# A hybrid decoder layer on one core: all x tiles loaded first, low parts of the k, v and u weights on GpSimd, k normed with a scaled epsilon, and the opening in written order

## The chip, the cores and the metric

The program runs on one core of a Trainium2 chip. A core has five engines that run their own instruction streams side by side: TensorE (PE in the profile; PEld is its weight load), VectorE (DVE), ScalarE (ACT), GpSimd (POOL) and SyncE (SP), which issues the DMAs here. They meet only at semaphores. The time is device microseconds of the whole launch, as the median of three runs.

## The reference, cut to what matters

One layer of a decoder on x of 1024 positions by 1024 features, in float32:

```python
h = rmsnorm(x, mix_norm)
q, k, v, su, sv, g_a, g_b = split(h @ w_in)          # 512,128,128,512,512,1024,1024 columns
y_att = sliding_window_attention(q, k, v, q_norm, k_norm, sinks)   # 8 query heads, 2 kv heads of 64
y_sgu = chunked_spatial_gating(su, sv, sgu_norm, w_s, b_s)
x = x + (sigmoid(g_a)*(y_att @ w_oa) + sigmoid(g_b)*(y_sgu @ w_ob)) @ w_out
x = x + conv_gated_mlp(rmsnorm(x, ffn_norm), w_up, conv_w, conv_b, w_down)
# inside the attention, per head of 64:
q = q * rsqrt(mean(q*q) + 1e-6) * q_norm
k = k * rsqrt(mean(k*k) + 1e-6) * k_norm
```

The change touches only the opening: the k and v columns of the projection, the norm of x (a row sum of squares), the norm of k, the first four query blocks, and what is prepared for the first scores.

## The kernel before, in words

**Float32 by three products.** Every operand is split into a high part, rounded to the matmul type (`copy_hi`, an ACT copy, line 89), and a low part, the rest (a subtraction on DVE or GpSimd). `mm3` (lines 91 to 95) then issues three matmuls: high by high, high by low, low by high.

**The x stage (lines 197 to 255).** x comes transposed in eight tiles of 128 features, k = 0 to 7. A tile `xr[k]` holds one column of gains, the 256 weight columns of k and v, and 1024 positions: 640.5 KB, loaded by `xload` on SP's queue. For each tile, ACT rounds the weights to `wkv` high and the gained x to `x` high in two halves; the low parts are line 230 (weights, DVE) and line 234 (x, DVE, a scalar_tensor_tensor that reads `xf` or `xr` and the high part). Then 24 matmuls of 128x256 add the tile's share of k and v into the two PSUM tiles `pkv`. `xsquare` squares the tile on ACT into PSUM (line 218) and DVE adds it to `sqsum`, which lies in `rstd_b` (line 219). Five tiles are loaded ahead (`X_AHEAD`); tiles 0 to 2 lie in one buffer of the pool `Y` (`xf`), 3 to 7 rotate through three buffers (`xr`). In this stage PE keeps its written order, and the order of the other engines is chosen by a scheduler; SP's queue is in that order too, and it starts with tile 3. Seven small matmuls `warm` run on PE before the first tile.

**Weights of the first queries and of u.** `rsplit` makes the two halves of `wq` (copy on ACT, low part of 128x1024 on GpSimd, line 193). The first tile of u is split at line 258 (ACT) and 259 (DVE).

**From there to the first scores (lines 317 to 420), in written order on all engines.** PE: the row sums of squares (`ssq`, line 321), `q_proj(0)` and `q_proj(1)` (24 matmuls each), four transposes of normed k (`pk`), `q_proj(2)`, transposes of the first two query blocks (`pqt`), the reciprocal norms as a row (`rb`, half 0), `q_proj(3)`, k's other half, `rb` half 1, and the first scores (`sc`, line 439). Beside it DVE and GpSimd make `rstd` (x's reciprocal norm), and from k's squares `kss` the factor `krs`: times `rstd` squared, plus epsilon, to the power -1/2 on GpSimd (line 131), times `rstd` again; line 348 applies it. `q_ms` does it for a query block with the scaled epsilon `eps_x` and no `rstd`: q's raw values carry the factor that cancels. `v_evac` takes v out of PSUM, `v_split` splits it; `k_hi`, `k_lo`, `k_twice` split k.

PSUM tiles of half size (`PH`, four buffers) hold the squares, `ssq`, `pq`, `pk`, `pqt` and `rb` in turn: a new one waits until an older one has been read. A DMA waits until the eighth DMA before it on the queue has landed.

Of the kernel before, what the change touches and what calls it, by code (L numbers as in the profile page):

```python
# [10 lines left out]
F = mybir.dt.float32  # L11
R = mybir.dt.float32r
# [6 lines left out]
D = 1024  # L19
# [3 lines left out]
EPS = 1e-6  # L23
# [5 lines left out]
ROWS = (slice(0, 64), slice(64, 128))  # L29
X_AHEAD = 5  # L30
FILL = "qu|q|qu|qu|uu|q|qu|qu|q|qu|qu|qu|q|uu|u|u|uu|vv|v|v".split("|")
# [10 lines left out]
def body(ctx, tc, nc, a):  # L42
# [157 lines left out]
    xr = {}  # L200
    x_first = Y("xf", F, [128, 3, 1281])

    def xload(k):
        xr[k] = x_first[:, k, :] if k < 3 else pa.tile([128, 1281], F, tag="xr", name=nm("xr"), bufs=3)
        if k == 0:
            nc.sync.dma_start(xr[k][:, 0:513], a["xw"][k, :, 0:513])
            nc.sync.dma_start(xr[k][:, 513:1281], a["xw"][k, :, 513:1281])
        else:
            nc.sync.dma_start(xr[k], a["xw"][k])
# [10 lines left out]

    for k in range(X_AHEAD):
        xload(k)
    warm = PH("warm")
    for _ in range(7):
        nc.tensor.matmul(warm[:, 0:128], rstd_b[:, 0:128], rstd_b[:, 0:128], start=True, stop=True)
    xcuts = {0: (slice(0, 256), slice(256, 512), slice(512, 1024))}
    for k in range(8):
        x1 = xr[k]
        copy_hi(wkv[:, 0, k, :], x1[:, 1:257])
        nc.vector.tensor_tensor(wkv[:, 1, k, :], x1[:, 1:257], wkv[:, 0, k, :].bitcast(F), op=ALU.subtract)  # L230
        for c in xcuts[k] if k in xcuts else (slice(0, 512), slice(512, 1024)):
# [4 lines left out]
        for s in range(8):  # L236
# [3 lines left out]
                k == 0 and s % 2 == 0, k == 7 and s % 2 == 1)  # L240
        if k > 0:
            xsquare(k - 1)
        if k + X_AHEAD < 8:
            xload(k + X_AHEAD)
        if k == 2:
            rwq = rload(a["wq"][0], "wq")
            nc.sync.dma_start(ident, a["ident"])
            nc.sync.dma_start(cp, a["cp"])
        if k == 4:
            u_raw = [wload(a["wu"][0], "wu")]  # L250
            nc.sync.dma_start(sink_b, a["sink"])
            nc.sync.dma_start(ali, a["ali"])
        if k == 5:
            rsplit(wq[0], rwq[0], 0)
    xsquare(7)
    rsplit(wq[0], rwq[1], 1)
    u_next = [wst.tile([128, 8, 128], R, tag="wh", name="u0h"), wst.tile([128, 8, 128], R, tag="wl", name="u0l")]
    copy_hi(u_next[0], u_raw[0])
    nc.vector.tensor_tensor(u_next[1], u_raw[0], u_next[0].bitcast(F), op=ALU.subtract)

# [51 lines left out]
    krs = pa.tile([128, 16], F, name="krs")  # L312
    rstd2 = pa.tile([128, 8], F, name="rstd2")
    kss3 = kss.rearrange("p (s g) -> p s g", g=2)
    krs3 = krs.rearrange("p (s g) -> p s g", g=2)

    man = tc.manual_schedule()
    man.__enter__()
    p_ssq = PH("ssq")
    for s in range(8):  # L320
        nc.tensor.matmul(p_ssq[:, 2 * s:2 * s + 2], sqsum[:, s * 128:(s + 1) * 128], ones,
                         start=True, stop=True)
    q_proj(0)
    q_proj(1)
    ss8 = pa.tile([128, 8], F, name="ss8")
    nc.vector.tensor_scalar(nsink, sink_b, -1.0, None, op0=ALU.mult)
    nc.vector.tensor_scalar(kgq, cp[:, 184:185], cp[:, 185:186], 0.125, op0=ALU.mult, op1=ALU.mult)
    nc.vector.tensor_copy(ss8, p_ssq[:, 0:16].rearrange("p (s two) -> p s two", two=2)[:, :, 0])
    rsqrt_cols(rstd, ss8, 8, D)
    nc.vector.tensor_scalar(eps_x, ss8, EPS / D, EPS * EPS, op0=ALU.mult, op1=ALU.add)  # L330
    ksqs = pa.tile([128, 8, 128], F, tag="sq", name="ksq")
    for h in range(2):
# [3 lines left out]
                                axis=AX.X, op=ALU.add)  # L336
    nc.vector.tensor_tensor(rstd2, rstd, rstd, op=ALU.mult)
    nc.vector.tensor_tensor(kss3, kss3, rstd2.unsqueeze(2).to_broadcast([128, 8, 2]), op=ALU.mult)
    rsqrt_cols(krs[:, 0:8], kss[:, 0:8], 8, 64)
    rsqrt_cols(krs[:, 8:16], kss[:, 8:16], 8, 64)  # L340
    q_sq(0)
    q_sq(1)

    def k_norm(h):
        ss = slice(4 * h, 4 * h + 4)
        nc.vector.tensor_tensor(krs3[:, ss], krs3[:, ss],
                                rstd[:, ss].unsqueeze(2).to_broadcast([128, 4, 2]), op=ALU.mult)
        nc.vector.tensor_tensor(kr[:, ss, :].rearrange("p s (g d) -> p s g d", d=64),
                                pk4[h][:, :, 0:128].rearrange("p s (g d) -> p s g d", d=64),
                                krs3[:, ss].unsqueeze(3).to_broadcast([128, 4, 2, 64]), op=ALU.mult)  # L350
# [38 lines left out]

    v_evac(0)  # L390
    k_norm(0)
    k_trans(0)
    q_ms(0)
    q_ms(1)
    k_hi(0)
    v_evac(1)
    q_norm(0)
# [20 lines left out]
    q_sq(3)
    q_ms(3)
# [1626 lines left out]
```

## Time and profile before

| what | value |
|---|---|
| median of three runs | 1184.44 us (1184.26 to 1184.85) |
| span of the profiled execution, first to last instruction | 1183.5 us |
| median less span | 0.9 us |
| PE busy | 1170.3 us, 99% |
| PE busy from 0 to 80 us | 75.4 us |
| first matmul of the x stage | 6.30 us |
| first matmul of `ssq` (end of the x stage) | 31.41 us |
| first matmul of the scores | 48.93 us |
| mean granted PE clock | 0.998 |

The profile lists the span of its execution and no launch time of its own; the 0.9 us lie before the first and after the last instruction. In the rows below, a timeline row gives start, duration, engine, source line, operation, output and inputs, shapes, count, and in brackets the idle time before it with what ended it. A windows row gives for a stretch of time each engine's busy time and instructions, the granted PE clock, the DMA share and GB/s. Durations of neighbouring instructions on DVE and ACT overlap by some 0.09 us, so that the step from start to start is shorter than the duration.

### The profile page before, as it was taken

What the parts mean: (1) busy time and instruction counts of PE and PEld (TensorE: products, weight loads), DVE (VectorE), ACT (ScalarE), POOL (GpSimd) and SP (SyncE); (2) the same over time, 40 slices, a digit from 0 to 9 for tenths busy, and PEclk for the clock granted to TensorE, in tenths of its full rate; (3) what the DMA queues carried; (4) which work ended last, traced back from release to release, by engine and by line L of the source; (5) the groups of instructions that cost most, each with busy time, mean ns of one, the idle gap of its engine ahead of it and who ended that gap; (6) DMA issues with size and microseconds to landing.
All of it is one profiled execution on the core that took longest, in us unless ns stands there. A gap on an engine that the chain in (4) does not pass through costs nothing.

```text
span 1183.5 us, 15928 instructions
## 1 busy us (share of the span) xinstructions
PE 1170.3 (99%) x5842; PEld 990.4 (84%) x5842; DVE 874.5 (74%) x1037; ACT 566.5 (48%) x878; POOL 631.8 (53%) x435
## 2 busy tenths in 40 slices
PE   8999999999999999999999999999999999999998
PEld 8989989988888878888878888888888888888887
DVE  7798975743536776678788788877888797875674
ACT  8555667644336653335444443444444445425331
POOL 2467685488884764444867677776767541000000
PEclk9999999999999999999999999999999999999999
DMA  7110136157556654454545445455555268975471
GB/s 272 37 55 19 54 130 228 56 168 239 161 160 204 233 193 154 146 176 132 138 129 169 118 149 152 142 141 134 166 137 160 72 219 287 365 232 196 155 231 67
DMA packets 80942, 188.66 MB, mean 159 GB/s; under 512 B 9184, under 2 KB 16864, under 8 KB 80736
## 3 DMA queue, kind: packets, MB, share of 16 engines
q1 hardware_dynamic: 73008, 167.58, 40.7%
q0 software_dynamic: 7456, 15.73, 8.0%
q10 hardware_dynamic: 400, 4.33, 1.1%
q8 instruction: 46, 0.75, 0.3%
q14 instruction: 32, 0.26, 0.1%
HBM read 146.97 MB, written 49.02 MB: 166 GB/s over the span
## 4 chain that ended last, share of the span: by engine, by line
PE 82%; DVE 4%; POOL 3%; ACT 2%; issue 2%; DMA 1%; DVEq 0%; POOLq 0%; SPq 0%; ACTq 0%
PE pz L1060 50%; PE pd L1855 10%; PE pdy L1855 8%; PE px L95 2%; PE px L93 2%; PE px L94 2%; PE pu L95 1%; PE pu L93 1%; PE pu L94 1%; PE pv L517 1%; PE pq L93 1%; PE pq L95 1%; PE pq L94 1%; DVE xa L621 1%; DMA lq<-wup 0%
## 5 line engine op out<-in xcount | busy, mean ns | idle before, releaser
L1060 PE MATMUL pz<-T,qh 128*128 128x512 f32 x472 | 145.6, 390 | 0.0
L1060 PE MATMUL pz<-B,ph 128*128 128x512 f32 x352 | 109.7, 393 | 0.7 <-ACT x L1695 0.7
L1060 PEld LDWEIGHTS pz<-T,qh 128*128 128x128 f32 x472 | 88.4, 188 | 18.6 <-ACT u L885 0.3
L1019 POOL TENSOR_TENSOR pl<-lp,ph 128x1024 fp32r<-128x1024 f32 x30 | 73.2, 2439 | 52.9 <-ACT ph L89 52.9
L1060 PE MATMUL pz<-T,ql 128*128 128x512 f32 x236 | 91.8, 389 | 0.0
L1019 POOL TENSOR_TENSOR ql<-lq,qh 128x1024 fp32r<-128x1024 f32 x30 | 76.8, 2559 | 9.1 <-ACT qh L89 9.1
L1060 PEld LDWEIGHTS pz<-B,ph 128*128 128x128 f32 x352 | 65.1, 188 | 16.7 <-ACT x L1695 3.8
L1078 DVE TENSOR_TENSOR pz<-pz,rstd_b 128x1024 f32<-128x1024 f32 x60 | 73.9, 1232 | 4.6 <-ACT rstd_b L143 2.5
L1060 PE MATMUL pz<-T,s3h 128*128 128x512 f32 x232 | 71.4, 389 | 0.0
L1060 PE MATMUL pz<-y,wjh 128*128 128x512 f32 x224 | 69.5, 391 | 0.6 <-POOL y L1233 0.3
L1060 PE MATMUL pz<-B,pl 128*128 128x512 f32 x176 | 68.6, 390 | 0.0
L1855 PE MATMUL pd<-bh,ah 128*128 128x512 f32 x176 | 68.5, 389 | 0.0
L1855 PE MATMUL pd<-bl,ah 128*128 128x512 f32 x176 | 68.5, 389 | 0.0
L1855 PE MATMUL pd<-bh,al 128*128 128x512 f32 x176 | 68.5, 389 | 0.0
L1060 PE MATMUL pz<-T,AX 128*128 128x512 f32 x264 | 63.4, 389 | 0.0
L1060 PE MATMUL pz<-B,AX 128*128 128x512 f32 x264 | 63.4, 389 | 0.0
L1019 POOL TENSOR_TENSOR s3l<-lq,s3h 128x512 fp32r<-128x512 f32 x20 | 26.0, 1298 | 62.3 <-ACT s3h L89 62.3
L1060 PEld LDWEIGHTS pz<-T,AX 128*128 128x128 f32 x264 | 49.5, 188 | 10.3
L1060 PEld LDWEIGHTS pz<-B,AX 128*128 128x128 f32 x264 | 49.6, 188 | 10.3
L89 ACT ACTIVATE AX<-lr 128x1024 fp32r<-128x1024 f32 x22 | 23.4, 1063 | 70.9 <-POOL lr L621 70.9
L621 DVE TENSOR_TENSOR pz<-pz,u 128x512 f32<-128x512 f32 x37 | 25.9, 700 | 42.5 <-ACT u L1072 36.2
L1550 DVE SCALAR_TENSOR_TENSOR tg<-pz,cp,tg 128x1023 f32<-128x1023 f32 (+1 forms) x44 | 56.2, 1278 | 0.8
(359 smaller groups left out, 3597.6 us busy)
## 6 DMA issues: line engine op xcount, KB each, us to landing
lp<-wup SPq DMA_DIRECT2D x22, 512.0 KB, 3.8
lq<-wup SPq DMA_DIRECT2D x22, 512.0 KB, 4.2
ra<-wdown SPq DMA_DIRECT2D x44, 256.0 KB, 4.9
b<-T SPq DMA_DIRECT2D x44, 256.0 KB, 3.5
lq<-wup POOLq DMA_DIRECT2D x42, 256.0 KB, 5.3
B<-tv SPq DMA_DIRECT2D x33, 256.0 KB, 2.0
T<-tt SPq DMA_DIRECT2D x33, 256.0 KB, 2.1
b<-B SPq DMA_DIRECT2D x33, 256.0 KB, 3.0
```

The source lines that it names most:

```text
L89: return nc.scalar.activation(dst, src, AF.Copy, scale=scale)
L93: nc.tensor.matmul(out, wh, mh, start=first, stop=False, **kw)
L94: nc.tensor.matmul(out, wh, ml, start=False, stop=False, **kw)
L95: nc.tensor.matmul(out, wl, mh, start=False, stop=last, **kw)
L517: nc.tensor.matmul(o, vhl[:, kb, g, :], w[:, 2 * g:2 * g + 2, :], start=i == 0 and g == 0, stop=i == len(ops) - 1, skip_group_check=True)
L621: eng.tensor_tensor(out, x, y, op=op)
L1019: nc.gpsimd.tensor_tensor(l, r, h.bitcast(F), op=ALU.subtract)
L1060: nc.tensor.matmul(o, p[:, k, :], m, start=not more and k == 0 and j == 0, stop=k == nk - 1 and j == 2, skip_group_check=True)
L1078: nc.vector.tensor_tensor(z, z, rstd_b, op=ALU.mult)
L1550: nc.vector.scalar_tensor_tensor(t[:, j:], p[:, 0:1024 - j], cw[:, ci, 2 - j:3 - j], t[:, j:], op0=ALU.mult, op1=ALU.add)
L1855: nc.tensor.matmul(o[d], p[:, k - k0, m], q[:, k - k0, :], start=new and k == 0 and j == 0, stop=k == HK - 1 and j == 2, skip_group_check= ...
```

## The change

- All eight tiles of x are loaded first, in order of k, the first six into two `Y` buffers, the last two into `xr`; then both halves of `wq`, and the small inputs and u's weights that were issued between the tiles.
- Eleven `warm` matmuls in place of seven.
- The low parts of the k and v weights of tiles 1 to 7, and of u's first weights, are made on GpSimd; tile 0's stay on DVE.
- The order of all engines is the written one from the first load on. The squares lag behind the tiles: the last three come after the second half of `wq`.
- `krs` is k's mean square plus `eps_x`, to the power -1/2, with no `rstd` in it: `rstd2` and the product with `rstd` are gone, and `rstd` itself is made later, on GpSimd after the two `krs` powers.
- `q_proj(0)` stands before `ssq`; `v_evac` moves behind the first two query blocks; both `rb` halves stand behind k's second half; u's first copy and subtraction move behind `q_proj(1)` and `v_evac`; the norm and the squares of blocks 2 and 3 stand earlier.

On GpSimd, from the last of the opening's fills on (`wkv` is the k and v weights' low part, `mh` the exponent -1/2). Before:

```order
L172 MEMSET kT_107 64x1024
L193 TENSOR_TENSOR wq_102<-wq_249,wq_102 128x1024
L193 TENSOR_TENSOR wq_102<-wq_251,wq_102 128x1024
L131 TENSOR_TENSOR rstd<-rstd,mh_74 128x8
L131 TENSOR_TENSOR krs<-krs,mh_74 128x8 x2
```

Now (line numbers of the changed kernel):

```order
L171 MEMSET kT_107 64x1024
L239 TENSOR_TENSOR wkv_120<-xf_126,wkv_120 128x256 x2
L239 TENSOR_TENSOR wkv_120<-xf_127,wkv_120 128x256 x3
L192 TENSOR_TENSOR wq_102<-wq_141,wq_102 128x1024
L239 TENSOR_TENSOR wkv_120<-xr_137,wkv_120 128x256
L239 TENSOR_TENSOR wkv_120<-xr_139,wkv_120 128x256
L192 TENSOR_TENSOR wq_102<-wq_143,wq_102 128x1024
L345 TENSOR_TENSOR krs<-krs,mh_74 128x8
L291 TENSOR_TENSOR qss_532<-qss_532,mh_74 128x4
L291 TENSOR_TENSOR qss_545<-qss_545,mh_74 128x4
L397 TENSOR_TENSOR krs<-krs,mh_74 128x8
L130 TENSOR_TENSOR rstd<-rstd,mh_74 128x8
```

The low part of `wq`'s first half now stands ahead of the weights' low parts of tiles 6 (`xr_137`) and 7 (`xr_139`), and the power for `krs` is cut into two with two query powers between them.

On VectorE at tiles 6 and 7. Before (`xr_209` is tile 6, `xr_247` tile 7):

```order
L230 TENSOR_TENSOR wkv_120<-xr_209,wkv_120 128x256
L234 SCALAR_TENSOR_TENSOR x_5_118<-xr_209,x_5_118 128x512
L234 SCALAR_TENSOR_TENSOR x_6_119<-xr_209,x_6_119 128x512
L219 TENSOR_TENSOR rstd_b<-rstd_b,sq_402 128x512
L230 TENSOR_TENSOR wkv_120<-xr_247,wkv_120 128x256
L219 TENSOR_TENSOR rstd_b<-rstd_b,sq_435 128x512
L234 SCALAR_TENSOR_TENSOR x_5_118<-xr_247,x_5_118 128x512
L234 SCALAR_TENSOR_TENSOR x_6_119<-xr_247,x_6_119 128x512
```

Now:

```order
L243 SCALAR_TENSOR_TENSOR x_5_118<-xr_137,x_5_118 128x512
L243 SCALAR_TENSOR_TENSOR x_6_119<-xr_137,x_6_119 128x512
L218 TENSOR_TENSOR rstd_b<-rstd_b,sq_397 128x512
L218 TENSOR_TENSOR rstd_b<-rstd_b,sq_400 128x512
L243 SCALAR_TENSOR_TENSOR x_5_118<-xr_139,x_5_118 128x512
L243 SCALAR_TENSOR_TENSOR x_6_119<-xr_139,x_6_119 128x512
```

The two weight subtractions are gone from DVE, and both additions of one tile's squares stand ahead of tile 7's low parts.

On ScalarE behind the x stage (`ksq` are k's squares, `qsq` those of a query block, `u0h` is u's first high part, `kT` k's). Before:

```order
L89 ACTIVATE wq_102<-wq_251 128x1024
L89 ACTIVATE u0h<-wu_327 128x1024
L334 ACTIVATE ksq<-pkv_124 128x512
L334 ACTIVATE ksq<-pkv_125 128x512
L276 ACTIVATE qsq_537<-pq_469 128x256
L276 ACTIVATE qsq_539<-pq_494 128x256
L89 ACTIVATE kT_107<-pk_544,kgq 64x512 x2
```

Now:

```order
L335 ACTIVATE ksq<-pkv_124 128x512
L335 ACTIVATE ksq<-pkv_125 128x512
L284 ACTIVATE qsq_526<-pq_460 128x256
L284 ACTIVATE qsq_536<-pq_493 128x256
L88 ACTIVATE u0h<-wu_147 128x1024
L88 ACTIVATE kT_107<-pk_540,kgq 64x512 x2
```

The copy of u's weights now stands between the second query block's squares and k's high part.

```diff
@@ -27,7 +27,6 @@
 
 
 ROWS = (slice(0, 64), slice(64, 128))
-X_AHEAD = 5
 FILL = "qu|q|qu|qu|uu|q|qu|qu|q|qu|qu|qu|q|uu|u|u|uu|vv|v|v".split("|")
 WHEN = {"u1": 0, "q0": 1, "q1": 2, "u2": 5, "u3": 9, "v0": 13, "v1": 14, "z0": 16, "z1": 17}
 
@@ -198,10 +197,10 @@
     pkv = [PS("pkv"), PS("pkv")]
     pk4 = [pkv[h].rearrange("p (s c) -> p s c", c=256) for h in range(2)]
     xr = {}
-    x_first = Y("xf", F, [128, 3, 1281])
+    x_first = [Y("xf", F, [128, 3, 1281]) for _ in range(2)]
 
     def xload(k):
-        xr[k] = x_first[:, k, :] if k < 3 else pa.tile([128, 1281], F, tag="xr", name=nm("xr"), bufs=3)
+        xr[k] = x_first[k // 3][:, k % 3, :] if k < 6 else pa.tile([128, 1281], F, tag="xr", name=nm("xr"), bufs=3)
         if k == 0:
             nc.sync.dma_start(xr[k][:, 0:513], a["xw"][k, :, 0:513])
             nc.sync.dma_start(xr[k][:, 513:1281], a["xw"][k, :, 513:1281])
@@ -218,16 +217,26 @@
             nc.scalar.activation(sq, xs, AF.Square)
             nc.vector.tensor_tensor(sqsum[:, c], sqsum[:, c], sq, op=ALU.add)
 
-    for k in range(X_AHEAD):
+    man = tc.manual_schedule()
+    man.__enter__()
+    for k in range(8):
         xload(k)
+    rwq = rload(a["wq"][0], "wq")
+    nc.sync.dma_start(ident, a["ident"])
+    nc.sync.dma_start(cp, a["cp"])
+    u_raw = [wload(a["wu"][0], "wu")]
+    nc.sync.dma_start(sink_b, a["sink"])
+    nc.sync.dma_start(ali, a["ali"])
     warm = PH("warm")
-    for _ in range(7):
+    for _ in range(11):
         nc.tensor.matmul(warm[:, 0:128], rstd_b[:, 0:128], rstd_b[:, 0:128], start=True, stop=True)
     xcuts = {0: (slice(0, 256), slice(256, 512), slice(512, 1024))}
-    for k in range(8):
+
+    def x_block(k):
         x1 = xr[k]
         copy_hi(wkv[:, 0, k, :], x1[:, 1:257])
-        nc.vector.tensor_tensor(wkv[:, 1, k, :], x1[:, 1:257], wkv[:, 0, k, :].bitcast(F), op=ALU.subtract)
+        eng = nc.gpsimd if k else nc.vector
+        eng.tensor_tensor(wkv[:, 1, k, :], x1[:, 1:257], wkv[:, 0, k, :].bitcast(F), op=ALU.subtract)
         for c in xcuts[k] if k in xcuts else (slice(0, 512), slice(512, 1024)):
             xc = x1[:, 257 + c.start:257 + c.stop]
             copy_hi(hx(0, k, c), xc, scale=x1[:, 0:1])
@@ -238,25 +247,24 @@
             c = slice(s * 128, (s + 1) * 128)
             mm3(o, hx(0, k, c), hx(1, k, c), wkv[:, 0, k, :], wkv[:, 1, k, :],
                 k == 0 and s % 2 == 0, k == 7 and s % 2 == 1)
-        if k > 0:
-            xsquare(k - 1)
-        if k + X_AHEAD < 8:
-            xload(k + X_AHEAD)
-        if k == 2:
-            rwq = rload(a["wq"][0], "wq")
-            nc.sync.dma_start(ident, a["ident"])
-            nc.sync.dma_start(cp, a["cp"])
-        if k == 4:
-            u_raw = [wload(a["wu"][0], "wu")]
-            nc.sync.dma_start(sink_b, a["sink"])
-            nc.sync.dma_start(ali, a["ali"])
-        if k == 5:
-            rsplit(wq[0], rwq[0], 0)
-    xsquare(7)
+
+    x_block(0)
+    x_block(1)
+    xsquare(0)
+    x_block(2)
+    x_block(3)
+    xsquare(1)
+    x_block(4)
+    xsquare(2)
+    x_block(5)
+    xsquare(3)
+    rsplit(wq[0], rwq[0], 0)
+    x_block(6)
+    xsquare(4)
+    x_block(7)
     rsplit(wq[0], rwq[1], 1)
-    u_next = [wst.tile([128, 8, 128], R, tag="wh", name="u0h"), wst.tile([128, 8, 128], R, tag="wl", name="u0l")]
-    copy_hi(u_next[0], u_raw[0])
-    nc.vector.tensor_tensor(u_next[1], u_raw[0], u_next[0].bitcast(F), op=ALU.subtract)
+    for k in (5, 6, 7):
+        xsquare(k)
 
     st = {}
 
@@ -310,41 +318,37 @@
     kr = pa.tile([128, 8, 128], F, tag="xr", name="kr", bufs=3)
     kss = pa.tile([128, 16], F, name="kss")
     krs = pa.tile([128, 16], F, name="krs")
-    rstd2 = pa.tile([128, 8], F, name="rstd2")
+    u_next = [wst.tile([128, 8, 128], R, tag="wh", name="u0h"), wst.tile([128, 8, 128], R, tag="wl", name="u0l")]
     kss3 = kss.rearrange("p (s g) -> p s g", g=2)
     krs3 = krs.rearrange("p (s g) -> p s g", g=2)
 
-    man = tc.manual_schedule()
-    man.__enter__()
     p_ssq = PH("ssq")
+    q_proj(0)
     for s in range(8):
         nc.tensor.matmul(p_ssq[:, 2 * s:2 * s + 2], sqsum[:, s * 128:(s + 1) * 128], ones,
                          start=True, stop=True)
-    q_proj(0)
     q_proj(1)
     ss8 = pa.tile([128, 8], F, name="ss8")
-    nc.vector.tensor_scalar(nsink, sink_b, -1.0, None, op0=ALU.mult)
-    nc.vector.tensor_scalar(kgq, cp[:, 184:185], cp[:, 185:186], 0.125, op0=ALU.mult, op1=ALU.mult)
-    nc.vector.tensor_copy(ss8, p_ssq[:, 0:16].rearrange("p (s two) -> p s two", two=2)[:, :, 0])
-    rsqrt_cols(rstd, ss8, 8, D)
-    nc.vector.tensor_scalar(eps_x, ss8, EPS / D, EPS * EPS, op0=ALU.mult, op1=ALU.add)
     ksqs = pa.tile([128, 8, 128], F, tag="sq", name="ksq")
     for h in range(2):
         ksq = ksqs[:, 4 * h:4 * h + 4, :]
         nc.scalar.activation(ksq, pk4[h][:, :, 0:128], AF.Square)
         nc.vector.tensor_reduce(kss[:, 8 * h:8 * h + 8], ksq.rearrange("p s (g d) -> p (s g) d", d=64),
                                 axis=AX.X, op=ALU.add)
-    nc.vector.tensor_tensor(rstd2, rstd, rstd, op=ALU.mult)
-    nc.vector.tensor_tensor(kss3, kss3, rstd2.unsqueeze(2).to_broadcast([128, 8, 2]), op=ALU.mult)
-    rsqrt_cols(krs[:, 0:8], kss[:, 0:8], 8, 64)
-    rsqrt_cols(krs[:, 8:16], kss[:, 8:16], 8, 64)
+    nc.vector.tensor_scalar(nsink, sink_b, -1.0, None, op0=ALU.mult)
+    nc.vector.tensor_scalar(kgq, cp[:, 184:185], cp[:, 185:186], 0.125, op0=ALU.mult, op1=ALU.mult)
     q_sq(0)
+    nc.vector.tensor_copy(ss8, p_ssq[:, 0:16].rearrange("p (s two) -> p s two", two=2)[:, :, 0])
+    nc.vector.tensor_scalar(eps_x, ss8, EPS / D, EPS * EPS, op0=ALU.mult, op1=ALU.add)
+    nc.vector.scalar_tensor_tensor(krs3, kss3, 1.0 / 64, eps_x.unsqueeze(2).to_broadcast([128, 8, 2]),
+                                   op0=ALU.mult, op1=ALU.add)
+    nc.gpsimd.tensor_tensor(krs[:, 0:8], krs[:, 0:8], mh05, op=ALU.pow)
+    q_ms(0)
     q_sq(1)
+    copy_hi(u_next[0], u_raw[0])
 
     def k_norm(h):
         ss = slice(4 * h, 4 * h + 4)
-        nc.vector.tensor_tensor(krs3[:, ss], krs3[:, ss],
-                                rstd[:, ss].unsqueeze(2).to_broadcast([128, 4, 2]), op=ALU.mult)
         nc.vector.tensor_tensor(kr[:, ss, :].rearrange("p s (g d) -> p s g d", d=64),
                                 pk4[h][:, :, 0:128].rearrange("p s (g d) -> p s g d", d=64),
                                 krs3[:, ss].unsqueeze(3).to_broadcast([128, 4, 2, 64]), op=ALU.mult)
@@ -387,13 +391,12 @@
             copy_hi(vh_, vg_)
             nc.vector.tensor_tensor(vl_, vg_, vh_.bitcast(F), op=ALU.subtract)
 
-    v_evac(0)
     k_norm(0)
     k_trans(0)
-    q_ms(0)
     q_ms(1)
+    nc.gpsimd.tensor_tensor(krs[:, 8:16], krs[:, 8:16], mh05, op=ALU.pow)
+    rsqrt_cols(rstd, ss8, 8, D)
     k_hi(0)
-    v_evac(1)
     q_norm(0)
     k_lo(0)
     q_norm(1)
@@ -404,18 +407,21 @@
     q_split(0)
     q_trans(1)
     q_split(1)
-    rms_rows([PH("rb")], rstd, (0,))
+    q_sq(2)
+    q_ms(2)
+    v_evac(0)
+    v_evac(1)
+    nc.gpsimd.tensor_tensor(u_next[1], u_raw[0], u_next[0].bitcast(F), op=ALU.subtract)
     q_proj(3)
     k_trans(1)
+    rms_rows([PH("rb")], rstd, (0,))
     rms_rows([PH("rb")], rstd, (1,))
-    q_sq(2)
+    k_hi(1)
+    q_norm(2)
+    k_lo(1)
+    q_sq(3)
     v_split()
-    q_ms(2)
-    k_hi(1)
-    k_lo(1)
     k_twice(1)
-    q_norm(2)
-    q_sq(3)
     q_ms(3)
     man.__exit__(None, None, None)
     pa_cm.__exit__(None, None, None)
```

## The prediction, made before the run

> **What bounds the kernel now.** I read the busy times first, then stretches of time, then PE's waits.
>
> ```profile
> PE 1170.3 (99%) x5842; PEld 990.4 (84%) x5842; DVE 874.5 (74%) x1037; ACT 566.5 (48%) x878; POOL 631.8 (53%) x435
> 4.40:6.30 1.90, 0.01 (x1) 0.00 (x0) 0.84 (x3) 1.23 (x3) 0.00 (x0) 1.00 1.05 323
> 6.30:8.20 1.90, 1.84 (x9) 1.23 (x9) 0.98 (x4) 1.18 (x3) 0.00 (x0) 1.00 0.90 331
> 8.20:11.60 3.40, 3.40 (x16) 3.40 (x17) 3.02 (x6) 3.40 (x8) 0.00 (x0) 0.50 1.00 405
> 11.60:31.40 19.80, 19.80 (x170) 19.80 (x169) 19.80 (x32) 18.76 (x34) 4.88 (x2) 1.00 0.64 233
> 31.40:49.00 17.60, 16.63 (x143) 16.26 (x141) 11.25 (x30) 6.07 (x12) 6.90 (x5) 1.00 0.18 62
> 130.00:1183.50 1053.50, 1045.81 (x4927) 873.26 (x4925) 766.02 (x808) 484.08 (x652) 564.18 (x361) 1.00 0.53 168
> PE pkv L93 <- ACT x L89: 1.9, 1, 1.9
> PE pqt L295 <- DVE krs L346: 0.6, 1, 0.6
> PE pq L93 <- DVE qs L304: 0.4, 1, 0.4
> ```
>
> PE sets the end: 1170.3 of 1183.5 us are busy, and the order of the work after 60 us is unchanged. So only idle or slow PE time in the opening can be won. The windows show it. From 4.4 to 6.3 PE does nothing (row `pkv`, 1.9 us). From 8.2 to 11.6 it is busy, but at a granted clock of 0.50. At full clock, 11.6 to 31.4, 170 matmuls take 19.8 us, 0.1165 each, so a tile's 24 take 2.80. The slow window held 16, worth 1.86, and cost 3.40: 1.54 lost. Behind the x stage, from 31.4 to 49, 0.97 us is idle, in the rows `pqt` and `pq`. All of it together is some 5 us, 0.4% of the time.
>
> **The start.** What limits it is the second tile.
>
> ```profile
> 1.06 3.35 PE L225 MATMUL warm<-rstd_b 128*128 128x128 f32 x14 [1.06 <-POOL mh L123]
> 7.02 1.12 ACT L89 ACTIVATE x<-xf 128x256 fp32r<-128x256 f32 x2 [0.77 <-DMA xf<-xw]
> 1.80:18.00 16.20, 14.26 (x92) 13.35 (x91) 11.24 (x21) 12.49 (x25) 1.82 (x3) 0.89 0.95 351
> L1295 POOL TENSOR_TENSOR wjl<-wj,wjh 128x256 fp32r<-128x256 f32 x8 | 5.9, 741 | 0.0
> L234 DVE SCALAR_TENSOR_TENSOR x<-xr,x 128x512 fp32r<-128x512 f32 x10 | 7.1, 744 | 0.4 <-ACT x L89 0.4
> ```
>
> Before, ACT reached tile 0's second piece when it landed, at 7.02, with tile 3 ahead of it on the queue: two tiles, 1.28 MB. Now these two places hold tiles 0 and 1, so I put tile 1's landing at 7.02 too. Tile 0 comes earlier. The warm matmuls took 3.35 us for seven (two records each), .48 each; four more end between 5.4, at twice that pace, and 6.3, so block 0 runs until 8.2 to 9.1. For block 1, ACT rounds the weights (.31) and the first half of x (.71): 8.04. GpSimd's low part takes .74 by the nearest operation of the same shape (row L1295). It and DVE's subtraction of x (.74) would run together; I put one behind the other (the reason is the next part), so block 1's third matmul starts at 8.97. The 22 behind it end at 11.54. Bounds: 10.9, the early end of block 0 and 23 matmuls, if the two run together; 12.3 if tile 1 lands .75 later among its seven companions. I take 11.54. PE no longer pauses 2 us ahead of block 0, and I count no half clock. Blocks 2 to 5 then end at 11.54 + 4 x 2.80 = 22.74. Before, PE was there at 31.41 - 2 x 2.80 = 25.81: 3.1 us are won up to here.
>
> **Two subtractions at a time.** This is the step on which the forecast turns. GpSimd now subtracts during the x stage, where DVE subtracts too.
>
> ```profile
> 21.75 2.44 POOL L193 TENSOR_TENSOR wq<-wq,wq 128x1024 fp32r<-128x1024 f32 x1 [18.05 <-ACT wq L89]
> 19.55 0.42 DVE L230 TENSOR_TENSOR wkv<-xr,wkv 128x256 fp32r<-128x256 f32 x1
> 23.05 1.42 DVE L230 TENSOR_TENSOR wkv<-xr,wkv 128x256 fp32r<-128x256 f32 x1
> 21.21 1.88 DVE L219 TENSOR_TENSOR rstd_b<-rstd_b,sq 128x512 f32<-128x512 f32 x3
> 61.29 1.04 POOL L481 TENSOR_TENSOR c<-c,sm 128x512 f32<-128x512 f32 x1 [0.40 <-DVE sm L480]
> 56.36 0.16 DVE L466 SCALAR_TENSOR_TENSOR sm<-sm,nsink 128x4 f32<-128x4 f32 x1
> 61.73 0.62 DVE L466 SCALAR_TENSOR_TENSOR sm<-sm,nsink 128x4 f32<-128x4 f32 x1
> ```
>
> While GpSimd subtracts `wq` from 21.75 to 24.19, DVE's weights subtraction takes 1.42 us in place of .42, and ends at 24.47, just behind it. A scalar_tensor_tensor does the same beside line 481: .62 in place of .16, ending at 62.35, .02 behind GpSimd's 62.33. The additions of squares (line 219), whose second input lies in PSUM, run beside the same `wq` subtraction at .63 each, unhindered. So a DVE operation with both inputs in SBUF waits for GpSimd's to end; I take the reverse too. The Trainium skill says the same in "SBUF — State Buffer", section "Who interferes with whom": a DVE instruction with two SBUF inputs contends with a GpSimd instruction that reads SBUF, and whoever issues first has the ports for the whole instruction. By that rule, which speaks against this change, the next paragraph holds; the rows above bear it out for DVE as the one that waits, and no row shows GpSimd waiting.
>
> Where it bites is set by ACT, which does one piece behind the other:
>
> ```profile
> 15.47 0.40 ACT L89 ACTIVATE wkv<-xr 128x256 fp32r<-128x256 f32 x1
> 17.00 1.10 ACT L218 ACTIVATE sq<-xr 128x512 f32<-128x512 f32 x2
> 18.04 0.40 ACT L89 ACTIVATE wkv<-xr 128x256 fp32r<-128x256 f32 x1
> 20.62 1.05 ACT L89 ACTIVATE wq<-wq 128x1024 fp32r<-128x1024 f32 x1
> 21.57 1.09 ACT L218 ACTIVATE sq<-xr 128x512 f32<-128x512 f32 x2
> ```
>
> From start to start a tile takes 17.00 - 15.47 = 1.53, its squares 1.04, a half of `wq` .95. From 7.02 on, six tiles' pieces (1 to 6), five pairs of squares and one half of `wq` lead to these times: `wq`'s first half rounded at 19.87, tile 6's pieces from 19.78 to 21.31, tile 7's from 22.35 to 23.88, `wq`'s second half at 24.92. The eight tiles and the half of `wq` are 5.65 MB, which at 351 GB/s from 1.8 us on have landed by 17.9, when ACT comes to it at 18.83; each us later than that costs one.
>
> GpSimd holds 19.95 to 22.39 with `wq`. Tile 6's first x subtraction on DVE, ready at 20.8, waits until then and ends at 23.0; GpSimd's weights subtraction for tile 6, behind `wq` on its queue, gets its turn from 22.97 to 23.71; the second x subtraction follows, to 24.4. Block 6's second matmul needs those weights: due at 22.87, it starts at 23.76, .9 late. Then DVE adds two pairs' halves (1.2 us) to 25.57. Tile 7's weights are subtracted by 25.14, and GpSimd goes straight on with `wq`'s second half to 27.58, so tile 7's first x subtraction waits until then and ends at 28.2: block 7's third matmul is due at 26.67 and starts at 28.25, 1.58 late. The x stage ends at 22.74 + 5.60 + .9 + 1.58 = 30.8, against 31.41 before: **-.6**. Bounds: 28.65 with no waiting anywhere but a few tenths of late pieces, and 32.5 with both waits and a half clock behind them.
>
> **From there to the first scores.**
>
> ```profile
> 33.28 0.17 DVE L328 COPY ss<-ssq 128x8 f32<-128x8 f32 x1 [0.68 <-PE ssq L321]
> 33.74 1.68 POOL L131 TENSOR_TENSOR rstd<-rstd,mh 128x8 f32<-128x8 f32 x1 [2.41 <-DVE eps_x L330]
> 36.11 3.25 POOL L131 TENSOR_TENSOR krs<-krs,mh 128x8 f32<-128x8 f32 x2 [0.69 <-DVE krs L130]
> 37.99 0.69 DVE L348 TENSOR_TENSOR kr<-pkv,krs 128x512 f32<-128x512 f32 x1
> 38.85 0.60 PE L355 MATMUL pk<-ident,kr 128*128 128x128 f32 x4
> 28.72 1.05 ACT L89 ACTIVATE u0h<-wu 128x1024 fp32r<-128x1024 f32 x1
> 39.49 1.39 ACT L89 ACTIVATE kT<-pk,kgq 64x512 fp32r<-64x512 f32 x2
> 40.99 1.50 DVE L369 SCALAR_TENSOR_TENSOR kT<-pk,kgq,kT 64x512 fp32r<-64x512 f32 x2
> 43.10 0.41 PE L295 MATMUL pqt<-ident,qr 128*128 128x128 f32 x2 [0.60 <-DVE krs L346]
> 48.93 0.36 PE L439 MATMUL sc<-kT,qs 128*128 128x256 f32 x1
> ```
>
> PE does `q_proj(0)`, `ssq` and `q_proj(1)` before `pk`. Before, from 31.41 to 38.85 that was 7.44 with no wait, so `pk` is now due at 30.8 + 7.44 = 38.25. The order inside is turned: `ssq` comes 2.8 us later, and the chain to k's norm starts at its end, when `q_proj(1)` starts, at 35.4. The changed chain is a copy (.17 behind the semaphore), `eps_x` (.21), `krs` (.21), one power of 1.64, k's norm (.69) and some .45 for the passages between engines (33.28 + .17 to 33.74 holds two operations and one): 38.75. So the power saved buys little, since `ssq` was moved behind `q_proj(0)`: `pk` waits .5 and stands at 38.75, against 38.85: **-.1**. This also eats .5 of the .6 won.
>
> Next, ACT has the copy of u's weights between the second query block's squares and k's high part: 38.45 + .3 + .95 = 39.70 (it was 39.49), then k's high part (1.39) to 41.09; DVE's low part (1.5) goes to 42.74, and the second block's norm, queued behind it, gives `pqt` at 43.3 against 43.10: **+.2**. Before, that copy lay at 28.72 under the x stage. Bounds: 0, if ACT gets to the copy .2 earlier, and +.5. `q_proj(3)` then starts without the wait of .4 (row `pq`), since `rb` no longer takes its PSUM buffer ahead of it; but both `rb` halves now stand between k's second half and the scores, with k's second half not ready before: some .3 (0 to .6). The first scores come at 43.3 + .25 + 4.16 + .9 + .3 = 48.95, with 4.16 for `q_proj(3)`, its evacuation wait and `k_trans`, and .9 for `rb`. Before: 48.93. So the x stage's gain is gone here.
>
> u's low part on GpSimd takes 2.44 by the `wq` row. It lies beside `q_proj(3)` and has some 2.8 us until u's first matmuls; without that cover it would cost up to 2.4. v's evacuation, moved behind the query blocks, and the norms of blocks 2 and 3, moved ahead, change DVE's queue before the third pair of scores by between -.8 and +.5; I take **+.1**. The sum: 48.95 - 48.93 + .1, about +.1. The profiled execution spans 1183.5; with .9 outside it, the median of the runs, the forecast is 1184.4 within its rounding.
>
> **Rivals.** *The subtractions do not hinder each other* in this pairing (GpSimd with a 128x256 or `wq` part, DVE with scalar_tensor_tensor of 128x512, which no row pairs). Then the x stage ends near 28.65, 2.8 us early; the chain behind `ssq` moves with it, and about 2.5 remain: 1181.9. Against it: both kinds wait in the rows above. *Only one wait bites*: `wq`'s second half is late, or DVE gets tile 7's first x subtraction in ahead of it. Block 7 does not wait, the x stage ends at 29.24, and -1.5 remains: 1182.9. For it: at tile 7 the order turns on .5 us. *Slower: the waits in blocks 6 and 7 halve the clock.* They are .9 and 1.6 us within 5.5. Before, 1.9 + .06 idle of the 3.8 us to 8.2 was followed by 3.40 us at 0.50, with 1.54 lost; a second such stretch puts the end at 1184.4 + 1.8 = 1186.2. [...] The Trainium skill, in "TensorE: Matmul & The Clock Gate", section "HAM oscillation — how this bites in real kernels", gives as its abstract rule that PE should have no idle gap over about 3.4 us; by that rule waits of .9 and 1.6 cost no clock, but here a pause of 1.9 was followed by 0.50, so the trace is stricter than the rule. *The change does not bring the early start*: tile 1 among seven companions lands at 8.5 rather than 7.02. ACT's chain and the end of the x stage move by up to 1.5: 1185.9. It counts with the slower cases.
>
> **How the numbers follow.** Forecast .62 (1184.4, own range 1183.3 to 1185.4, from the bounds of the start, `pqt`, `rb` and DVE's queue); no hindrance .14; one wait .12; half clock .07; late tile 1 .05. Less than 0.2%, 2.37 us, cannot be told from no change here, so faster means under 1182.07 and slower over 1186.81. Faster: .6 of the second case, a quarter of the third and some of the forecast's edge: .17. Slower: a third of the last two and some of the edge: .07. Same: .76. The range, 1182.0 to 1186.3, leaves out half of the no-hindrance case and the far ends of the slower ones.
>
> **What would show it.** Right: no clock of 0.50 between 8 and 12; low parts of x at tiles 6 and 7 that last about 2 us or more in place of .74, ending with GpSimd's `wq` rows; PE waits near 23 and 27 of about .9 and 1.6 for them; the first `pq` near 30.8; a wait of some .5 ahead of `pk`; the first scores near 48.9. Wrong: x's low parts all at .74 beside a running GpSimd subtraction, or tile 1 later than 7.5, or a window behind 23 at 0.50, or first scores more than 1 us off 48.9.

## The result and the profile after

The changed kernel is slower: 1187.72 us, median of 6 runs (1187.01 to 1191.08), beside 1184.2 us for the kernel before, also of 6 (1183.3 to 1184.85). The ratio is 1.0032, 95% interval 1.0021 to 1.0043: 3.5 us lost, where no change was forecast.

The opening first. The windows of the changed kernel (columns as in the prediction):

```profile
4.40:8.20 3.80, 3.80 (x28) 3.80 (x27) 1.80 (x4) 1.34 (x4) 0.00 (x0) 1.00 1.00 395
8.20:11.60 3.40, 3.04 (x24) 2.62 (x23) 1.75 (x3) 3.40 (x8) 1.14 (x2) 1.00 1.01 410
11.60:31.70 20.10, 18.29 (x154) 17.89 (x154) 19.15 (x24) 17.80 (x34) 9.60 (x8) 1.00 0.65 242
49.00:62.00 13.00, 12.09 (x93) 11.32 (x92) 9.08 (x21) 10.34 (x26) 6.35 (x5) 1.00 0.14 40
215.00:225.00 10.00, 7.86 (x55) 7.04 (x55) 8.91 (x14) 6.86 (x11) 1.42 (x2) 1.00 0.35 107
225.00:1186.00 961.00, 955.44 (x4247) 788.74 (x4245) 695.84 (x685) 420.63 (x515) 509.16 (x304) 1.00 0.55 170
```

PE no longer pauses from 4.4 to 6.3, and from 8.2 to 11.6 it has the full clock: the early start is there. 1.8 us are lost again between 11.6 and 31.7. And a stretch that the prediction took only as part of a longer one, 215 to 225, shows PE idle for 2.1 of 10 us. The same work in the kernel before:

```profile
214.00:224.00 10.00, 9.48 (x64) 8.55 (x63) 8.91 (x14) 6.83 (x10) 1.41 (x2) 1.00 0.34 107
217.12 0.75 DVE L760 SCALAR_TENSOR_TENSOR vg<-pvs,vss,sg_b 128x512 f32<-128x512 f32 x1
220.73 0.75 DVE L760 SCALAR_TENSOR_TENSOR vg<-pvs,vss,sg_b 128x512 f32<-128x512 f32 x1
219.75 0.63 PE L1060 MATMUL pz<-x,ph 128*128 128x512 f32 x2
```

PE's waits in the changed kernel (us in total, times, longest), and the rows at the new one:

```profile
PE pkv L94 <- DVE x L243: 1.6, 2, 1.4
PE pz L1066 <- DVE vg L766: 1.6, 1, 1.6
PE pqt L303 <- DVE qr L297: 1.0, 1, 1.0
PE sc L445 <- DVE c L464: 0.9, 1, 0.9
PE pkv L93 <- POOL wkv L239: 0.4, 1, 0.4
221.67 0.75 DVE L766 SCALAR_TENSOR_TENSOR vg<-pvs,vss,sg_b 128x512 f32<-128x512 f32 x1
222.47 0.73 PE L1066 MATMUL pz<-x,ph 128*128 128x512 f32 x2 [1.62 <-DVE vg L766]
```

Where a loss of PE is given below without a row, it is counted from start to start of two neighbouring matmuls, less the usual step of some .11; that gives .1 to .3 us more than the waits in these rows.

Before, the first `pz` product of the merge started at 219.75, between VectorE's last two reads of the v tiles (`pvs`). Now it waits for the last of them, which ends at 222.42. All engines have the same instructions in the same order there. What differs is where things lie. The four PSUM tiles of half size (`PH`) lie in one pool; when the v stage ends, that pool is closed and two double buffers are opened in its place, the first for the spatial gate's sums, the second for `pz`. A bank is here a numbered place in PSUM that holds one small tile, and a double buffer takes two. The built programs give these banks, 4 to 7, to the last four v tiles:

```
              pvs 4  pvs 5  pvs 6  pvs 7     first pz
before          5      7      6      4       6 and 7
changed         5      4      6      7       6 and 7
```

As the built programs show it, each small tile takes one of the banks that were handed back, so the order in which the opening's tiles are taken and handed back sets a rotation that later tiles inherit. The change put `ssq`, `pq`, `pqt` and `rb` in another order, and some 170 us later the last v tile lies under the first `pz`. In the kernel before, the first `pz` takes the place of `pvs` 5 and 6 alone.

### The profile page after: what moved, and what is told of

Its sections match the earlier page's. It is cut to its first block, busy times and chain, and to the rows that moved or that the text cites. A ratio compares the mean times of both kernels' runs of the same rounds, so it can differ in the third digit from the quotient of the medians.

```text
span 1186.1 us, 15941 instructions
## 1 busy us (share of the span) xinstructions
PE 1170.3 (99%) x5850; PEld 990.5 (84%) x5850; DVE 872.5 (74%) x1024; ACT 566.9 (48%) x878; POOL 639.6 (54%) x443
## 4 chain that ended last, share of the span: by engine, by line
PE 79%; DVE 8%; POOL 2%; issue 2%; ACT 2%; DMA 1%; SPq 0%; DVEq 0%; ACTq 0%; POOLq 0%
PE pz L1066 52%; PE pdy L1861 8%; PE pd L1861 7%; PE px L94 2%; PE px L92 2%; PE px L93 2%; DVE xa L627 1%; PE pu L94 1%; PE pu L92 1%; PE pu L93 1%; DVE ya L536 0%; PE pq L92 0%; DMA ra<-wdown 0%; DVE sm L472 0%; PE pq L94 0%
## 5 line engine op out<-in xcount | busy, mean ns | idle before, releaser
L88 ACT ACTIVATE ah<-ra 128x1024 fp32r<-128x1024 f32 (+1 forms) x24 | 23.7, 989 | 70.5 <-DMA ra<-wdown 23.0
L1556 DVE SCALAR_TENSOR_TENSOR tv<-pz,cp,tv 128x1023 f32<-128x1023 f32 (+1 forms) x44 | 56.2, 1278 | 0.8
```

The costliest lines, as they stand in the source:

```text
L88: return nc.scalar.activation(dst, src, AF.Copy, scale=scale)
L1556: nc.vector.scalar_tensor_tensor(t[:, j:], p[:, 0:1024 - j], cw[:, ci, 2 - j:3 - j], t[:, j:], op0=ALU.mult, op1=ALU.add)
```

## The experiments

They ran in three groups, each beside the kernel before (medians 1184.13, 1184.42 and 1184.37 us), the third on another chip.

### The rotation, taken out of the changed kernel

```diff
-    warm = PH("warm")
-    for _ in range(11):
+    for warm in [PH("warm")] * 5 + [PH("warm")] * 2 + [PH("warm")] * 2 + [PH("warm")] * 2:
```

> The changed kernel; the only edit is that its eleven warm matmuls write four small PSUM tiles in turn, not one, so that the four small PSUM buffers are handed on in another rotation. The last v tile (pvs 7) then lies in the first of the two double buffers that are made of them, as in the kernel before, not in the second, which the first pz takes. Theory A (the extra 1.8 us near 220 us is that PSUM rotation): the row of pz waiting for DVE's vg (1.6 us in the changed kernel) is gone, and the time falls by 1.6 to 1.9 us, to about 1186.0. Rival B (the wait belongs to late operands of the first pz): it stays, and the time stays at 1187.7.

Measured: 1186.22 us (11 runs), ratio to before 1.0016 (1.0007 to 1.0025); 1.5 us under the changed kernel, just short of the 1.6 to 1.9 expected. The row of `pz` for `vg` is gone, and `pz` starts right behind `pm`:

```profile
219.38 0.75 DVE L765 SCALAR_TENSOR_TENSOR vg<-pvs,vss,sg_b 128x512 f32<-128x512 f32 x1
222.02 0.63 PE L1065 MATMUL pz<-x,ph 128*128 128x512 f32 x2
```

### The rotation, put into the kernel before

```diff
-    warm = PH("warm")
-    for _ in range(7):
+    for warm in [PH("warm")] * 5 + [PH("warm")] * 2:
```

> The kernel before; the only edit is that two of its seven warm matmuls write a second small PSUM tile, so that the last v tile lies in the half of PSUM that the first pz takes, as in the changed kernel. Theory A: the first pz now waits some 1.8 us for DVE's vg near 219.7 us, and the kernel before becomes 1.6 to 1.9 us slower, about 1186.0. Rival B: no change, 1184.2.

Measured: 1186.24 us (11 runs), ratio 1.0018 (1.001 to 1.0027), 2.1 us over the kernel before, with the same row:

```profile
220.81 0.75 DVE L759 SCALAR_TENSOR_TENSOR vg<-pvs,vss,sg_b 128x512 f32<-128x512 f32 x1
221.61 0.73 PE L1059 MATMUL pz<-x,ph 128*128 128x512 f32 x2 [1.62 <-DVE vg L759]
```

Theory A holds in both directions: in the kernel before, two warm matmuls that write elsewhere cost 2 us, 215 us later.

### All small subtractions back on VectorE

```diff
-        eng = nc.gpsimd if k else nc.vector
+        eng = nc.vector
```

> The first of these runs with all low parts of the k and v weights on VectorE, none on GpSimd. Theory C (VectorE's low parts of x at tiles 6 and 7 wait for GpSimd's subtraction of wq, whoever does the small weights): the waits of PE at about 23.9 (0.6) and 27.5 us (1.5) stay within 0.5 us in sum, and the time stays within 0.6 us of the first run. Rival D (the small subtractions on GpSimd are what is late): both waits are gone, the x stage ends some 2 us earlier, and the time falls by 1.5 to 2 us.

Measured: 1187.78 us (5 runs), 1.6 us over the first run of this group, which it edits. The waits stay: PE loses 3.1 us in blocks 6 and 7, against 2.7 in the first run. They only change their owner, since VectorE's weights subtraction now stands behind GpSimd's `wq`:

```profile
20.24 2.44 POOL L192 TENSOR_TENSOR wq<-wq,wq 128x1024 fp32r<-128x1024 f32 x1 [16.53 <-ACT wq L88]
20.50 2.47 DVE L238 TENSOR_TENSOR wkv<-xr,wkv 128x256 fp32r<-128x256 f32 x1
25.30 2.40 POOL L192 TENSOR_TENSOR wq<-wq,wq 128x1024 fp32r<-128x1024 f32 x1 [2.62 <-ACT wq L88]
25.41 2.58 DVE L238 TENSOR_TENSOR wkv<-xr,wkv 128x256 fp32r<-128x256 f32 x1
```

What takes .42 us alone takes 2.5 here. Rival D falls. Theory C holds for the waits, but the time missed its bounds (within .6 us of the first run): .4 of the 1.6 us are seen in the two blocks. In the one profile PE also waits 1.4 us more near 594 and 1002 us than in the first run's, at two places whose waits come and go in most kernels here; whether that is the rest of the difference between the medians stays open.

### wq behind the last x block

The first run of the group with:

```diff
-    rsplit(wq[0], rwq[0], 0)
     x_block(6)
     xsquare(4)
     x_block(7)
+    rsplit(wq[0], rwq[0], 0)
     rsplit(wq[0], rwq[1], 1)
```

> The first of these runs with both halves of wq split behind the last x block, so that GpSimd's two subtractions of 128x1024 do not run beside VectorE's low parts of x. Theory C: PE's waits at tiles 6 and 7 are gone but for 0.1 to 0.2, VectorE's low parts there take 0.75 us each, the x stage ends near 29.6 in place of 31.7, and the time falls by 1.5 to 2.1 us against the first run. Rival D: the waits stay, no gain.

Measured: 1183.45 us (11 runs), ratio to before .9996 (.9987 to 1.0005), 2.8 us under the first run. The subtractions now take turns, and PE waits for none of them in blocks 6 and 7:

```profile
20.98 0.74 POOL L238 TENSOR_TENSOR wkv<-xr,wkv 128x256 fp32r<-128x256 f32 x1 [1.94 <-ACT wkv L88]
21.66 1.41 DVE L242 SCALAR_TENSOR_TENSOR x<-xr,x 128x512 fp32r<-128x512 f32 x2
24.18 1.41 DVE L242 SCALAR_TENSOR_TENSOR x<-xr,x 128x512 fp32r<-128x512 f32 x2
25.73 4.83 POOL L192 TENSOR_TENSOR wq<-wq,wq 128x1024 fp32r<-128x1024 f32 x2 [1.44 <-ACT wq L88]
```

The x stage ends at 29.44, though tile 1 came late in this execution (8.64). Theory C holds; the gain is .7 us more than its bound. `q_proj(0)` comes to the second half of `wq` some 1.4 us after that, at 30.8, and GpSimd is done with it at 30.56.

### The copy of u's weights moved early

The run before with:

```diff
+    copy_hi(u_next[0], u_raw[0])
     for h in range(2):
         ksq = ksqs[:, 4 * h:4 * h + 4, :]
...
     q_sq(1)
-    copy_hi(u_next[0], u_raw[0])
```

> The run with wq late (PSUM rotation as in the kernel before, both halves of wq split behind the last x block), and ScalarE's copy of u's first weights moved from behind the second query block's squares to ahead of k's squares. Theory (the copy delays k's high part, so k's low part, so the second query block's norm behind it on VectorE): k's high part starts .6 us earlier, PE's wait for the second pqt falls from 1.1 to about .5 us, and the time by .3 to .6 us. Rival (k's high part waits for the transposed k anyway): the wait stays at 1.1.

Measured: 1183.27 us (10 runs), ratio .9994 (.9985 to 1.0003). PE's wait for the second `pqt` falls from 1.12 to .70 us from start to start (.5 was expected). The waits show it as 1.0 and 0.5, first for the run before, then for this one:

```profile
PE pqt L302 <- DVE qr L296: 1.0, 1, 1.0
PE pqt L302 <- DVE qr L296: 0.5, 1, 0.5
```

In time it is .2 us, or .5 when each run is set against its own group's kernel before. The mechanism is there, the size in time cannot be told from nothing.

### The second block's norm ahead of k's low part

The changed kernel with `wq` late as above, its single warm tile, and:

```diff
-    k_lo(0)
     q_norm(1)
+    k_lo(0)
```

> The changed kernel with two edits: both halves of wq split behind the last x block, and the second query block's norm ahead of k's low part on VectorE (with one warm tile the PSUM rotation then puts the last v tile into the first double buffer by itself). Theory (the wait for the second pqt is the queue place of that norm behind 1.5 us of k's low part): PE's wait of 1.1 us for the second pqt is gone, k's low part ends .4 us later and is still ahead of the first scores, and the time is 0.8 to 1.1 us under the run with wq late, about 1182.5. Rival (the norm's factor from GpSimd comes late): the wait stays above .6 us.

Measured: 1182.70 us (11 runs), ratio .9988 (.9979 to .9997): .75 us under the run with `wq` late, or 1.0 when each run is set against its own group's kernel before (.8 to 1.1 expected). The wait of 1.1 us is gone, as the four transposes in one row show:

```profile
39.35 0.42 DVE L297 TENSOR_TENSOR qr<-pq,qss 128x256 f32<-128x256 f32 x1 [0.72 <-POOL qss L291]
39.77 1.51 DVE L373 SCALAR_TENSOR_TENSOR kT<-pk,kgq,kT 64x512 fp32r<-64x512 f32 x2
40.54 0.60 PE L303 MATMUL pqt<-ident,qr 128*128 128x128 f32 x4
```

Of the 1.1 us, .45 come back at once as a wait ahead of `q_proj(3)` and .2 in front of `rb`. Moving this one operation turned the PSUM rotation again: in the built program the plain single warm tile gives the last v tile bank 5, and four warm tiles would give it bank 7.

### The row sums of squares ahead of the first projection

The run with `wq` late, with the sixteen `ssq` matmuls moved ahead of `q_proj(0)`.

> The run with wq late, and the row sums of squares again ahead of the first query projection on PE, as in the kernel before. The prediction held that k's shorter chain buys little because the sums were moved behind that projection. If that is what costs, PE's wait ahead of pk (.4 us) goes and nothing takes its place: .4 us faster. Rival (the last squares are added at about 30.8, 1.4 us after the x stage ends, so the projection covers them): PE waits some 1.4 us for them, and the run is about 1 us slower.

Measured: 1184.13 us (10 runs), ratio .9995 (.9985 to 1.0004), .7 us over the run with `wq` late, within the scatter of both. The profile decides:

```profile
28.99 1.86 PEld L326 LDWEIGHTS ssq<-ones,rstd_b 128*128 128x128 f32 x16 [0.90 <-PE pkv L94]
```

PE waits .9 us for the squares, the wait of .4 ahead of `pk` is gone, and the wait for the second `pqt` grows from 1.12 to 1.56. From the end of the x stage to the first scores it takes .9 us longer. The projection covers the squares: the rival holds in its mechanism, with .9 us of waiting in place of its 1.4.

### The kernel before, once more

> The kernel before, unedited, for one more profile of it: whether the half clock from 8.2 to 11.6 us and PE's wait of 1.9 us ahead of it come back, and how far the launch's time lies above the span. If the 0.9 us taken for that is right, time less span is 0.9; if it was taken from an execution that was itself slower than the median, it is near the 1.7 us of the changed kernel's runs.

Measured: span 1183.1, time 1184.80: 1.7 us lie outside the span, as in the changed kernel (1187.79 against 1186.1). The .9 us of the prediction compared the span of one execution with the median of others; with the same 1.7 the profiled one had run at an estimated 1185.2. The pause of 1.9 us and the half clock (0.51 from 8.2 to 11.6) come back, and the first scores are at 48.63.

### Tile 1 in two pieces, u's copy early, and both

On top of the run with the norm first:

```diff
-        if k == 0:
+        if k < 2:
             nc.sync.dma_start(xr[k][:, 0:513], a["xw"][k, :, 0:513])
```

> The run with wq late and the second norm first, and tile 1 of x loaded in two pieces (weights and a quarter of x, then the rest), as tile 0 is. Theory (a load of 640 KB that shares the queue with its followers lands late because of its own size; a smaller piece in the same place lands earlier): ScalarE reaches tile 1's weights before 7.2 us (8.0 to 8.8 in the runs with one piece), PE waits under .5 us in block 1 in place of .8 to 1.8, and the time falls by .3 to .8 us. Rival (the queue serves loads in the order of issue, whatever their size): no change in block 1 and in the time.

> The run with wq late and the second norm first, with ScalarE's copy of u's first weights ahead of k's squares. Theory: now that PE no longer waits for the second pqt, the copy's place moves only k's high and low part, which nothing waits for until the first scores: within .4 us of the run without it (1182.7). Rival: ScalarE's queue still sets the wait of PE ahead of the fourth query projection (.45 us); then .4 to .6 us faster.

> Both edits of the two runs before together. If they act on different places they add: .3 to 1.2 us under 1182.7, about 1182.0, the fastest of all; it is meant as the version that beats both kernels.

Measured: tile 1 split 1181.23 us (9 runs), ratio .9974 (.9964 to .9984); u's copy early 1182.94 (11 runs), .9989 (.998 to .9997); both 1181.98 (11 runs), .9982 (.9973 to .999). The split brings 1.5 us over the run with the norm first, which ran in the group before, and 1.0 us where u's copy is early in both versions; .3 to .8 was expected. ScalarE reaches tile 1's weights at 5.61, and its x at 7.09, in place of 8.78 for all of it in the run with the norm first, the latest of all. First the split, then that run:

```profile
5.61 0.40 ACT L88 ACTIVATE wkv<-xf 128x256 fp32r<-128x256 f32 x1
7.09 1.34 ACT L88 ACTIVATE x<-xf 128x512 fp32r<-128x512 f32 x2 [1.08 <-DMA xf<-xw]
8.65 0.39 PE L94 MATMUL pkv<-wkv,x 128*128 128x256 f32 x1 [0.28 <-DVE x L243]
```

```profile
4.80 1.12 ACT L88 ACTIVATE x<-xf 128x256 fp32r<-128x256 f32 x2 [0.47 <-DMA xf<-xw]
8.78 0.42 ACT L88 ACTIVATE wkv<-xf 128x256 fp32r<-128x256 f32 x1 [2.86 <-DMA xf<-xw]
```

PE loses .45 us in block 1 with the split and 1.8 without. The runs of the split alone lie within 1.7 us and those of the run with the norm first within 4.6; but with the split and u's copy they lie within 3.4, so a smaller scatter is not shown. u's copy has no effect of its own that can be told from nothing, and the intervals of the two versions with the split overlap. Both together met the expected 1182.0, but not as a sum of two gains. The version with the split alone is the fastest that ran, 3.1 us under the kernel before and 6.4 under the changed one.

### The changed kernel, once more

> The changed kernel, unedited, on the same chip as the three runs before it, for a second profile of it: the wait of 1.8 us near 220 us comes back whole; PE's wait in block 1 (.8 us) differs by up to 1 us with the landing of tile 1; time 1187 to 1188.5.

Measured: 1187.67 us (4 runs), ratio 1.0035 (1.0021 to 1.0048). Tile 1 came at 7.28, near the 7.02 of the prediction, and the opening can be laid beside the forecast:

```profile
20.26 2.43 POOL L192 TENSOR_TENSOR wq<-wq,wq 128x1024 fp32r<-128x1024 f32 x1 [2.58 <-ACT wq L88]
21.14 3.23 DVE L243 SCALAR_TENSOR_TENSOR x<-xr,x 128x512 fp32r<-128x512 f32 x2 [0.74 <-ACT x L88]
23.87 0.38 PE L93 MATMUL pkv<-wkv,x 128*128 128x256 f32 x1 [0.93 <-POOL wkv L239]
25.32 2.42 POOL L192 TENSOR_TENSOR wq<-wq,wq 128x1024 fp32r<-128x1024 f32 x1 [0.36 <-ACT wq L88]
25.48 3.47 DVE L243 SCALAR_TENSOR_TENSOR x<-xr,x 128x512 fp32r<-128x512 f32 x2
28.34 0.39 PE L94 MATMUL pkv<-wkv,x 128*128 128x256 f32 x1 [1.35 <-DVE x L243]
31.04 0.28 PE L92 MATMUL pq<-wq,x 128*128 128x256 f32 x1
48.99 0.48 PE L445 MATMUL sc<-kT,qs 128*128 128x256 f32 x2
221.87 0.73 PE L1066 MATMUL pz<-x,ph 128*128 128x512 f32 x2 [1.62 <-DVE vg L766]
```

## Why the prediction was wrong

**What failed** is a sentence of its first part: "the order of the work after 60 us is unchanged. So only idle or slow PE time in the opening can be won." The order is unchanged, but a tile's place in PSUM is inherited from the opening, and with it the instruction that a later tile waits for. This costs 1.7 to 1.9 us of PE time in each profile that has it, and 1.5 and 2.1 us in the medians of the two runs that take it out and put it in. It stood in no term, bound or rival.

**The subtractions in turn** were right within .4 us in sum. Forecast: block 6 late by .9 and block 7 by 1.58, 2.5 us in all. Measured: .6 and 1.5 in the first profile, 1.1 and 1.5 in the second. VectorE's first x subtraction of tiles 6 and 7 waits for GpSimd's `wq`, and the reverse, which the prediction took without a row for it, stands in the first profile: GpSimd's weights subtraction, .64 us alone, takes 1.05 while VectorE's run.

```profile
11.67 3.23 DVE L243 SCALAR_TENSOR_TENSOR x<-xf,x 128x512 fp32r<-128x512 f32 x4 [0.83 <-ACT x L88]
12.64 1.05 POOL L239 TENSOR_TENSOR wkv<-xf,wkv 128x256 fp32r<-128x256 f32 x1 [0.90 <-ACT wkv L88]
```

This is what the Trainium skill says in "SBUF — State Buffer", section "Who interferes with whom", of two engines that hold the ports for a whole instruction in turn. Moving `wq` away won 2.8 us, so the conflict is the largest loss inside the opening; the forecast had it in its sum.

**Tile 1's landing** was mis-sized. I put it at 7.02, the time of the third load before. But that load was 384 KB and tile 1 is 640 KB: in nine profiles with tile 1 in one piece ScalarE reached it at 6.95 to 8.78, in the changed kernel's own two at 8.03 and 7.28. In the two profiles with the split its smaller first piece, in the same place on the queue, was reached at 5.61 and 6.99; what scatters these times is not shown. The x stage ended at 31.73 and 31.04, against 30.8 forecast and 31.41 before. My bound of .75 late was too short for the first profile, and the rival of a late tile 1 (8.5) came two thirds true in it.

**From the x stage to the scores** the sums hold within .3 us. Forecast were 18.15 us from the end of the x stage to the first scores; it took 17.85 and 17.95, and 17.4 to 17.5 before. With the x stage at 31.04 the scores came at 48.99 (48.95 forecast): the nearness is partly luck, since the x stage was .2 late and this stretch .2 short. With 31.73, they came at 49.57. Of the single terms, `pk` waits .4 (forecast .5), and the second `pqt` waits, as forecast, for a norm that stands late; the wait is 1.1 us because this norm stands behind k's low part, which I had in the chain but did not see as the one to move. Ahead of the third pair of scores (near 60 us) another .3 us was lost where I took .1: PE waits .9 for VectorE's `c` there, and .6 before. Three slips in the working change nothing: the terms of 48.95 add up to 48.91; its 4.16 is the time from `q_proj(3)` to the first scores before (44.77 to 48.93) and so holds one half of `rb`, and the .9 the other; the tiles and half of `wq` that are put at 5.65 MB are 5.77 MB, landed by 18.2 at the same rate, still ahead of 18.83.

**The half clock** is gone, by the earlier first tile or by the four more warm matmuls, which no run separates, and the waits in blocks 6 and 7 did not bring another. In the second profile of the changed kernel the stretch with both waits, 2.3 of 7 us idle, has the full clock:

```profile
22.00:29.00 7.00, 4.71 (x39) 4.32 (x38) 7.00 (x7) 5.29 (x10) 5.38 (x4) 1.00 0.24 81
29.00:33.00 4.00, 4.00 (x36) 4.00 (x35) 4.00 (x7) 2.25 (x4) 0.00 (x0) 1.00 0.38 129
```

That rival falls. Idle for half of the 3.8 us to 8.2, PE lost its full clock in the kernel before; idle for a third of these 7 us, it did not; where between them it turns, no run here shows. The rival without hindrance and the one with a single wait fall too: both waits are there.

**The baseline.** The profiled execution of before was itself an estimated .8 us over the median, and so only .9 seemed to lie outside the span, not 1.7. This did not move the forecast, which counts from the median, but it is why the first two profiles differ by 2.6 us and the medians by 3.5.

**The whole difference.** The second profiles of both kernels differ by 2.8 us, and the starts of the same matmuls show where it arises: .4 at the first scores, .3 more at the third, 1.9 more at the first `pz`, and another .4 near 243 us, which no experiment touched. There a later `pz` waits for ScalarE's `u` in every profile with the changed opening, and in none of the three with the old one:

```profile
PE pz L1066 <- ACT u L891: 0.2, 1, 0.2
```

It is there with either rotation, so it is another loss past 60 us that the sentence above put at nothing. Its cause stays open. These make 3.0 us; PE's waits near 593 us (0 to 1.3) and near 1000 us (0 to .9), which come and go in the profiles of most of the kernels, give back .2 in this pair. The medians differ by 3.3 in that group; the other .5 is what the two executions happened to be off their medians.

## What to carry to other kernels

When an opening is rearranged, "the rest is the same" has to be read from the places of the tiles too, not from the instructions alone: compare which bank each PSUM tile gets, and what was last there, wherever a pool is closed and its space taken over. A long GpSimd subtraction placed among VectorE's operations with both inputs in SBUF holds them up, and the other way round: here two of 2.4 us cost PE 2.1 to 2.9 us. Put it where VectorE reads PSUM, as with `wq` behind the last x block. A load that the pipeline waits for should be small, also where many larger ones are queued behind it: the split of tile 1 brought 1.0 to 1.5 us.

## What the runs showed that was not expected

- Two of seven warm matmuls that write another PSUM tile cost 2.1 us (1186.24 against 1184.13), 215 us after they ran.
- The load of tile 1, third on the queue and 640 KB, was reached between 6.95 and 8.78 us in nine executions of kernels that load alike. The x stage moves with it: it ended 23.7 to 23.8 us behind it in the changed kernel's two profiles and the one with its rotation taken out, and 20.8 us behind it in four of the five with `wq` late and tile 1 in one piece (21.5 in the fifth).
- After 1.9 us of pause PE had lost half its clock for 3.4 us in the kernel before, in both of its profiles (granted 0.50 and 0.51); waits of 1.1 and 1.5 us within 6 us cost the changed kernel none (1.00).
